# Seven inner products for P4 of the last output block in a pooling mixer

## The chip, the cores and the metric

The kernel runs on one core of a Trainium2 chip, as one launch. The metric is the device time of one execution in microseconds.

## The reference

The model is one layer of a streaming encoder trunk for x of 4096 rows and 1024 columns, float32. With one layer only the pooling mixer is used, not the gated attention:

```python
normed = rms_norm(x, norm_w)
u, gate = split(normed @ in_w, 2)                 # in_w 1024 x 2048
pooled = trailing means of u (windows 2, 4, 8, 16 for the four column groups) - u
mixed = einsum('bsgc,gcd->bsgd', pooled, group_w) + group_b
y = mixed * scale * silu(gate)
h = x + y @ out_w                                 # out_w 1024 x 1024
out = rms_norm(h, final_norm_w)
```

The change touches only `y @ out_w` for the last 512 rows.

## The kernel before

**Arithmetic.** All large matrix products are done with numbers split in two parts (a high part rounded to the matmul's input type, and the rest), as three matmuls: high by high, high by low, low by high. `split` (L232) makes the two parts with an ACT copy and a DVE subtraction; `copy` (L227) and `on_vector` (L213) are the helpers whose lines L229 and L215 stand in the profile for all such work.

**Stages.** A first stage folds weights together. Then come the phases "a" and "b" (the input projection in two column halves, four blocks of 1024 rows), with pooling beside them, and then the output phase "o", eight blocks (0 to 7) of 512 rows. Every block of every phase is a product of 2 x 2 blocks in Strassen's way with seven products P1 to P7 in place of eight. In the output phase their order is P1, P7, P6, P2, P5, P4, P3 (`ORDER_OUT`, L39), and each product multiplies 256 rows of some sum of quarters of y by a 512 x 512 sum of quarters of `out_w`, kept split in `w[i]`.

**A plain product.** `product_out` (L864) does two row halves of 128 rows (j = 0, 1). Each has four blocks of the contracted dimension and three matmuls for each, with 512 columns moving: 24 matmuls, all through `mm3` (L783).

**An inner product.** For the products named in `INNER` (L32), from one block to another, the same product is once more cut in 2 x 2 and done as seven inner products: A11 B11, A12 B21, S4 B22, A22 T4, S1 T1, S2 T2, S3 T3. The left sums S1 to S4 are made in phase "b" and kept in DRAM (`inner_sums`, `sumd`); the right sums T1 to T4 are made once (`inner_rights`, `split_inner`). T1 to T3 lie in buffers of their own. T4 is written over the quarter B12 (A22 B22's partner that the seven products don't need) of `w[i][0]`. Each inner product is six matmuls with 256 columns moving (`mm_inner`, L967, matmul on L972). The first, A11 B11, is issued by `inner_first` (L985) between the row halves of the product ahead, and ACT copies its result to a second bank. `inner_rest` (L992) issues the other six, and then adds the shared parts to the output rows with six `add_quarter` (L978, DVE on L980, 128 x 256 each), ahead of the ordinary eviction. For the shared parts P4 uses the two PSUM banks in which P1 and P2 were summed, once P2 is evicted; P2 uses the two spare banks.

Before the change `INNER` says that P2 is done so in blocks 1 to 7 and P4 in blocks 2 to 6. In block 7 P4 is a plain product and needs its quarter B12 back in place of T4. So behind P1 of block 7 `load_b12` (L912) loads it from DRAM, and behind P6 `split_b12` (L917) splits it into its place:

```python
def split_b12(i):
    src, t = raw_quarter(i, 0, 1), b12_place(i)
    for k in range(2):
        copy(t[:, 0, k], src[k])
        sub(t[:, 1, k], src[k], t[:, 0, k].bitcast(F32))
    give(inner_w[i].pop(("raw", 0)))
```

**What runs ahead.** `steps` lists all products. At step n the loads for up to step n + 4 are issued (`load_reach`, `load_o` L1182), and the left operands are formed and split for up to step n + 2 (`split_reach` L1698, `split_o` L1205). An inner P4 is an exception: its left side is split only one step ahead, and with it the sums S1 to S4, which `load_o` has loaded when it came to P3's step. A plain left side takes one of four `ops` buffers in turn, an inner one two of them. The order of instructions on each engine comes from a scheduler, which may put later work of the program ahead of work that isn't ready; the code above only sets priorities and dependencies.

**Buffers.** Rows and sums lie in two pools of equal tiles (`st`, `vt`), and `take` hands out the one given back longest ago; a new load waits until the old content has been read.

**The end.** `evict_o` (L1355) adds a product from PSUM to the rows x (L1373, DVE, one for each row half). In blocks 0 to 6 the row norm is computed behind P4 and P3 by `square_rows`. In block 7 it is done in parts to shorten the end: behind P2 and P5 `early_half` squares half rows on ACT (L1303) and multiplies them by the final weight on DVE, and behind P4 and P3 `square_part`, `late_factor` (root on ACT, L1321; small DVE operations, L1296 and L1324 to L1326), `late_scalar` (ACT, L1335) and `late_vector` (DVE, L1345) finish the rows and send them. P4 completes one 256-row half of the block (two groups of 128 rows), and P3 the other. P3's second row half is done in two column halves, the last one in a spare bank.

Of the kernel before, what the change touches and what calls it, by code (L numbers as in the profile page):

```python
# [28 lines left out]
NV = 8  # L29
EPS = 1e-6  # L30
FIRST_INNER = 1
INNER = {2: (1, 7), 4: (2, 6)}  # L32
INNER_IN = (0,)
STORED = {3: (0, 1, 2, 3)}

P1, P2, P3, P4, P5, P6, P7 = range(1, 8)
# [56 lines left out]
def kernel(  # L93
# [138 lines left out]
    def split(dst, src):  # L232
# [15 lines left out]
    wid = {  # L248
        i: [dram.tile([P, 2, H], F32, name=f"wid{i}_{n}") for n in range(2)] for i in INNER
    }  # L250
# [88 lines left out]
    def store_weights(dst, h, b11, b21, b12, b22):  # L339
        nc.sync.dma_start(out=dst[P1][h], in_=b11)  # L340
        nc.sync.dma_start(out=dst[P2][h], in_=b21)
        if h and P2 in INNER and dst is wod:
            inner_rights(P2, b21)
        for i, u in combine(b11, b21, b12, b22).items():
            nc.sync.dma_start(out=dst[i][h], in_=u)
            if h and i in INNER and dst is wod:
                inner_rights(i, u)
# [77 lines left out]
    def inner_rights(i, low):  # L425

        high, more = take(), take()
        nc.sync.dma_start(out=high, in_=wod[i][0])
        b11, b12, b21, b22, t4, t2 = (
            u.rearrange("p k (s a) -> p k s a", s=2)[:, :, :, c * QW : (c + 1) * QW] for u in (high, low, more) for c in range(2)  # L430
        )
        sub(b11, b12, b11)
        sub(b12, b22, b12)
        sub(t2, b22, b11)
        sub(t4, b21, t2)
        for n, u in enumerate((high, more)):
            nc.sync.dma_start(out=wid[i][n], in_=u)
            give(u)
# [454 lines left out]
    def is_inner(b, i):  # L893
        return i in INNER and INNER[i][0] <= b <= INNER[i][1]

    inner_w = {i: {} for i in INNER}

# [807 lines left out]
    def row_plan(b):  # L1705
# [19 lines left out]
        (2, P7): [(split_inner, P4, "T3")],  # L1725
        (2, P6): [(split_inner, P4, "T2")],
        (2, P2): [(split_inner, P4, "T4"), (end_inner, P4)],
        (7, P1): [(load_b12, P4)],
        (7, P6): [(split_b12, P4)],
    }  # L1730

    for n in range(2, len(steps)):
# [163 lines left out]
```

## Time and profile before

| | us |
|---|---|
| median of three runs | 906.63 |
| lowest and highest run | 905.44, 909.16 |
| the profiled execution's own time | 905.18 |
| its span, from the first to the last instruction | 903.4 |

PE is TensorE's matmuls, PEld its weight loads, DVE VectorE, ACT ScalarE, POOL GpSimd, and SP the engine that issues most transfers. A row of a timeline gives the start and the duration in microseconds, the engine, the line, the operation with what it writes and reads, how many of them, and in brackets how long the engine had been idle before it and what ended that. A row of the chain of waits gives start, duration and what the chain ran through. A row of a table by windows gives, for each stretch, its length, the busy time of PE, PEld, DVE, ACT and POOL with their numbers of instructions, the granted TensorE clock as a share of full speed, the busy share of the DMA engines and GB/s. A row of the list of transfers gives what is written from what, the queue, how many, the size of each, and the median time from issue to landing.

Matmuls are pipelined, so the durations of single ones overlap; what a group of them costs is read from where the next group starts.

### The profile page before, as it was taken

What the parts mean: (1) busy time and instruction counts of PE and PEld (TensorE: products, weight loads), DVE (VectorE), ACT (ScalarE), POOL (GpSimd) and SP (SyncE); (2) the same over time, 40 slices, a digit from 0 to 9 for tenths busy, and PEclk for the clock granted to TensorE, in tenths of its full rate; (3) what the DMA queues carried; (4) which work ended last, traced back from release to release, by engine and by line L of the source; (5) the groups of instructions that cost most, each with busy time, mean ns of one, the idle gap of its engine ahead of it and who ended that gap; (6) DMA issues with size and microseconds to landing.
All of it is one profiled execution on the core that took longest, in us unless ns stands there. A gap on an engine that the chain in (4) does not pass through costs nothing.

```text
span 903.4 us, 12068 instructions
## 1 busy us (share of the span) xinstructions
PE 895.7 (99%) x4482; PEld 790.3 (87%) x4482; DVE 776.2 (86%) x973; ACT 487.6 (54%) x807; POOL 42.0 (5%) x75
## 2 busy tenths in 40 slices
PE   9999999999999999999999999999999999999997
PEld 7888888888888888898888888888898998999996
DVE  5999994894998998699589589799999989889897
ACT  6979547447346556355445545654446435355354
POOL 0023101101100000000000000000100000000000
PEclk9999999999999999999999999999999999999999
DMA  9986966956856844056826866855875584584652
GB/s 349 408 320 198 347 221 193 316 187 230 335 207 228 280 146 140 24 154 225 326 89 224 331 236 215 291 194 190 278 254 203 188 308 147 180 279 158 216 187 94
DMA packets 75148, 205.40 MB, mean 227 GB/s; under 512 B 6928, under 2 KB 29840, under 8 KB 75088
## 3 DMA queue, kind: packets, MB, share of 16 engines
q1 hardware_dynamic: 67440, 179.17, 56.3%
q10 hardware_dynamic: 5040, 16.79, 5.0%
q0 software_dynamic: 2608, 8.66, 2.7%
q8 instruction: 35, 0.57, 0.3%
q14 instruction: 25, 0.20, 0.1%
HBM read 130.13 MB, written 74.46 MB: 226 GB/s over the span
## 4 chain that ended last, share of the span: by engine, by line
PE 98%; DVE 1%; ACT 0%; issue 0%; DVEq 0%; ACTq 0%
PE bank L783 87%; PE bank L972 6%; PE bank L497 3%; PE bank L816 1%; PE bank L1485 0%; DVE op L215 0%; DVE w L215 0%; DVE st L215 0%; PE bank L563 0%; ACT vt L1303 0%; DVE st L1373 0%; DVE st L1345 0%; ACT vt L1335 0%; ACT vt L229 0%; DVEq L1892 0%
## 5 line engine op out<-in xcount | busy, mean ns | idle before, releaser
L783 PE MATMUL bank<-op,w 128*128 128x512 f32 x2640 | 571.4, 379 | 0.2
L783 PEld LDWEIGHTS bank<-op,w 128*128 128x128 f32 x2640 | 498.4, 189 | 72.3 <-DVE op L215 1.0
L783 PE MATMUL bank<-w,op 128*128 128x512 f32 (+1 forms) x1068 | 232.2, 377 | 0.0
L783 PEld LDWEIGHTS bank<-w,op 128*128 128x128 f32 x1068 | 198.3, 189 | 26.9 <-issue 0.2
L215 DVE TENSOR_TENSOR op<-st,op 128x1024 fp32r<-128x1024 f32 x79 | 95.2, 1209 | 28.5 <-ACT op L229 28.3
L229 ACT ACTIVATE op<-st 128x1024 fp32r<-128x1024 f32 x79 | 82.4, 1048 | 57.5 <-PE bank L783 45.0
L229 ACT ACTIVATE op<-vt 128x1024 fp32r<-128x1024 f32 x69 | 71.8, 1052 | 58.4 <-PE bank L783 32.4
L215 DVE TENSOR_TENSOR op<-vt,op 128x1024 fp32r<-128x1024 f32 x69 | 83.6, 1215 | 10.4 <-ACT op L229 10.3
L229 ACT ACTIVATE vt<-bank 128x512 f32<-128x512 f32 x94 | 53.2, 590 | 44.3 <-PE bank L783 32.5
L229 ACT ACTIVATE bank<-bank 128x512 f32<-128x512 f32 (+1 forms) x76 | 38.0, 502 | 63.4 <-PE bank L783 32.1
L215 DVE TENSOR_TENSOR op<-s_st,op 128x1024 fp32r<-128x1024 f32 x31 | 37.6, 1217 | 12.0 <-ACT op L229 12.0
L229 ACT ACTIVATE op<-s_st 128x1024 fp32r<-128x1024 f32 x31 | 32.4, 1049 | 21.9 <-PE bank L783 11.8
L1373 DVE TENSOR_TENSOR vt<-bank,vt 128x512 f32<-128x512 f32 x56 | 37.9, 680 | 3.3 <-PE bank L783 3.3
L972 PE MATMUL bank<-w,op 128*128 128x256 f32 x288 | 40.0, 275 | 0.0
L972 PEld LDWEIGHTS bank<-w,op 128*128 128x128 f32 x288 | 37.8, 192 | 1.3
L215 DVE TENSOR_TENSOR vt<-bank,vt 128x512 f32<-128x512 f32 x50 | 32.7, 683 | 6.9 <-PE bank L783 6.8
L1237 POOL TENSOR_SCALAR oms<-oss 128x2 f32<-128x2 f32 x14 | 9.8, 696 | 615.4 <-ACT st L1264 443.2
L1070 DVE TENSOR_TENSOR_SCAN vt<-vt,bf 128x512 f32<-128x512 f32 x28 | 34.4, 1267 | 1.3 <-ACT vt L229 1.3
L215 DVE TENSOR_TENSOR w<-st,w 128x1024 fp32r<-128x1024 f32 (+2 forms) x25 | 28.1, 1132 | 8.5 <-ACT w L229 8.5
L229 ACT ACTIVATE w<-st 128x1024 fp32r<-128x1024 f32 (+2 forms) x25 | 24.2, 984 | 18.8 <-DMA st<-wod 9.0
L215 DVE TENSOR_TENSOR vt<-vt,vt 128x1024 f32<-128x1024 f32 (+1 forms) x29 | 33.0, 1140 | 0.1
L229 ACT ACTIVATE st<-bank 128x512 f32<-128x512 f32 x34 | 20.0, 594 | 24.0 <-PE bank L783 16.2
(171 smaller groups left out, 817.9 us busy)
## 6 DMA issues: line engine op xcount, KB each, us to landing
st<-in_x SPq DMA_DIRECT2D x27, 512.0 KB, 5.8
st<-in_xt SPq DMA_DIRECT2D x27, 512.0 KB, 8.9
vt<-in_x SPq DMA_DIRECT2D x27, 512.0 KB, 5.0
sd<-st ACTq DMA_DIRECT2D x27, 512.0 KB, 5.6
vt<-yd SPq DMA_DIRECT2D x18, 512.0 KB, 5.6
st<-sd SPq DMA_DIRECT2D x17, 512.0 KB, 5.4
out<-vt SPq DMA_DIRECT2D x17, 512.0 KB, 3.5
yd<-st SPq DMA_DIRECT2D x16, 512.0 KB, 2.9
```

Of the source, the lines that this page charges most:

```text
L215: made.append(nc.vector.tensor_tensor(out=dst, in0=a, in1=b, op=op))
L229: made.append(nc.scalar.activation(dst, src, func, **how))
L497: latest[0] = nc.tensor.matmul(ps2[kk][:, j * 256 : (j + 1) * 256], a[:, kk, 2 * j + t, :], maps if len(pairs) == 1 else woven(maps), star ...
L783: latest[0] = nc.tensor.matmul(ps, a, b, start=start and n == 0, stop=stop and n == 2, skip_group_check=True).ins
L816: latest[0] = nc.tensor.matmul(quarter_bank(banks_[c], n), a[:, x_, k, c * P : (c + 1) * P], right[:, y_, k], start=start and k + m == 0, ...
L972: latest[0] = nc.tensor.matmul(dst, a[k][x_], b[k][y_], start=start and k + n == 0, stop=k == 1 and n == 2, skip_group_check=True,).ins
L1070: nc.vector.tensor_tensor_scan(s[:, j, at:end], v[:, j, at:end], v[:, j, at - win : end - win], sums_of[j] if sums_of else 0.0, ALU.add, A ...
L1237: nc.gpsimd.tensor_scalar(out=ms, in0=ss, scalar1=-0.5 / D, scalar2=-0.5 * EPS, op0=ALU.mult, op1=ALU.add)
L1373: partial["added"] = nc.vector.tensor_tensor(out=dst, in0=src, in1=dst, op=ALU.add).ins
```

## The change

P4 of block 7 is done as seven inner products too, like P4 of blocks 2 to 6, and the load and the split of its quarter B12 are left out, since nothing reads that quarter any more.

```diff
-INNER = {2: (1, 7), 4: (2, 6)}
+INNER = {2: (1, 7), 4: (2, 7)}
...
         (2, P2): [(split_inner, P4, "T4"), (end_inner, P4)],
-        (7, P1): [(load_b12, P4)],
-        (7, P6): [(split_b12, P4)],
     }
```

By `is_inner(7, P4)`, which is now true, four more things follow in block 7: `load_o` loads S1 to S4 for P4, `split_o` splits them into a second `ops` buffer, `split_reach` lets P4's left side be split one step ahead in place of two, and P5's `product_out` issues `inner_first` between its row halves. The rest, from `evict_o` on, is the same code. Blocks 0 to 6 are the same.

## The prediction

> **What bounds the kernel now.** I read the page first, for the share of each engine, then the chain of waits for the stretch that the change touches, and then the timeline of VectorE (DVE) and ScalarE (ACT) in that stretch.
>
> ```profile
> span 903.4 us, 12068 instructions
> ...
> PE 895.7 (99%) x4482; PEld 790.3 (87%) x4482; DVE 776.2 (86%) x973; ACT 487.6 (54%) x807; POOL 42.0 (5%) x75
> ```
>
> TensorE (PE) is busy for 99% of the span, so a matmul taken out is worth its full time as long as nothing new makes PE wait, and as long as what follows the last matmul doesn't grow. The span is 903.4 us in an execution whose own time is 905.18 us; the median of the three runs is 906.63 us, 1.45 us above that execution. I make the sum as a difference and put it on the median.
>
> The end of the chain of waits shows both parts of the last output block, the matmuls and what comes after them.
>
> ```profile
> 873.75 0.67 PE bank L972 x6
> 874.42 2.59 PE bank L783 x12
> 877.01 4.02 PE bank L972 x36
> 881.03 12.97 PE bank L783 x60
> 893.99 0.02 issue
> 894.02 0.70 DVE st L1373
> ...
> 894.74 0.73 ACT vt L1303 x2
> ...
> 898.80 0.35 DVE s_st L1345
> ```
>
> Columns are start, duration, engine and line. L972 is the inner form (six matmuls 256 wide for each inner product), L783 the plain one (512 wide). The 60 plain matmuls from 881.03 are P5 (24), P4 (24) and the first row half of P3 (12). There the chain leaves PE: from 893.99 to the last DVE operation at 898.80 the kernel waits for evictions, squares and scales, not for matmuls, though the second row half of P3 still runs. So this block has two limits: PE up to the middle of P3, and DVE with ACT after it. The change is good for the first and must be weighed in the second.
>
> **The matmuls.** Twelve plain matmuls take 2.59 us (874.42), so P4 now costs 2 x 2.59 = 5.18 us. As inner products it costs 0.67 us (the first product, put between the row halves of P5) and 4.02 us (the other six), 4.69 us by the rows at 873.75 and 877.01. Saved: 5.18 - 4.69 = **0.49 us**. With these prices the new PE clock reads: P5's first row half ends at 881.03 + 2.59 = 883.62, the first inner product at 884.29, P5 at 886.88, P4 at 890.90 and P3's first row half at 893.49 instead of 893.99.
>
> A 256-wide matmul costs slightly more than half of a 512-wide one here (4.02/36 = 112 ns against 2.59/12 = 216 ns), and that it pays at all hangs on this. The Trainium skill, TensorE: Matmul & The Clock Gate, section Back-to-back issue gap, speaks against it: it says that in a stream of weight loads and matmuls the spacing is about 81 ns at 128 columns and 131 ns at 512. Interpolated, that gives an estimate of 98 ns at 256, so 42 x 98 against 24 x 131 ns, 0.97 us lost in place of 0.49 us gained, and a sum 1.46 us higher than mine. The rows above have both widths in the same stream and contradict it, so I give it no weight.
>
> **What is left out.** The load of the weight quarter (one transfer of 512 KB on SP's queue) and its split, two ACT copies and two DVE subtractions.
>
> ```profile
> 871.04 0.72 ACT L229 ACTIVATE w<-vt 128x256 fp32r<-128x256 f32 x2 [4.41 <-DMA vt<-wod]
> 871.55 1.53 SPq L1278 DMA_DIRECT2D out<-vt  x2
> ```
>
> The copies take 0.72 us on an ACT that had been idle for 4.41 us waiting for that very transfer, and the chain holds nothing but PE there, so leaving all of it out gains nothing that ends last. I take zero; if DVE were behind, the two subtractions would be worth as much as two of the 128x256 adds below, under 0.9 us.
>
> **What is added before P4: the sums S1 to S4.** One load of 512 KB, one ACT copy and one DVE subtraction of 128x1024. The load is issued at the P6 step, four steps ahead. By the order in which buffers are given back it gets the buffer of one of block 6's output rows, which are sent at 871.55 (second row above); it cannot start before that transfer has read it. The page and the list of transfers give the medians of such a store and of such a load:
>
> ```profile
> out<-vt SPq DMA_DIRECT2D x17, 512.0 KB, 3.5
> ...
> vt<-sumd SPq DMA_DIRECT2D x9, 512.0 KB, 4.4
> ```
>
> So it can start at about 871.6 + 3.5 = 875.1 and land at 875.1 + 4.4 = 879.5. Behind it on SP's queue are only the final stores, so nobody else waits. The split of A11 to A22 also moves, from two steps ahead to one. The ACT rows of blocks 6 and 7 show what that does:
>
> ```profile
> 841.55 1.07 ACT L229 ACTIVATE op<-vt 128x1024 fp32r<-128x1024 f32 x1 [2.01 <-PE bank L783]
> ...
> 845.00 1.06 ACT L229 ACTIVATE op<-vt 128x1024 fp32r<-128x1024 f32 x1 [1.53 <-PE bank L972]
> ```
>
> ```profile
> 876.83 1.06 ACT L229 ACTIVATE op<-vt 128x1024 fp32r<-128x1024 f32 x1 [1.72 <-PE bank L783]
> ...
> 880.33 1.06 ACT L229 ACTIVATE op<-vt 128x1024 fp32r<-128x1024 f32 x1 [1.58 <-PE bank L972]
> 883.18 0.63 ACT L1303 ACTIVATE vt<-st 128x512 f32<-128x512 f32 x1 [1.79 <-DVE st L1373]
> ...
> 885.29 0.63 ACT L1303 ACTIVATE vt<-s_st 128x512 f32<-128x512 f32 x1 [1.39 <-issue]
> ...
> 890.08 0.63 ACT L1303 ACTIVATE vt<-vt 128x512 f32<-128x512 f32 x1 [1.54 <-DVE vt L1373]
> ...
> 892.21 0.64 ACT L1303 ACTIVATE vt<-vt 128x512 f32<-128x512 f32 x1 [1.08 <-DVE vt L1373]
> ...
> 894.74 0.64 ACT L1303 ACTIVATE vt<-st 128x512 f32<-128x512 f32 x1 [0.86 <-DVE st L1373]
> ...
> 895.50 0.30 ACT L1321 ACTIVATE columns<-columns 128x1 f32<-128x1 f32 x1
> 895.70 0.71 ACT L1335 ACTIVATE vt<-vt,columns 128x512 f32<-128x512 f32 x1
> 896.31 0.40 ACT L1303 ACTIVATE vt<-s_st 128x256 f32<-128x256 f32 x1
> ...
> 896.83 0.72 ACT L1335 ACTIVATE st<-st,columns 128x512 f32<-128x512 f32 x1
> 897.48 0.42 ACT L1303 ACTIVATE vt<-s_st 128x256 f32<-128x256 f32 x1
> ```
>
> Block 6 has the late split (P4 is inner there), block 7 the early one, and yet the copy of P4's left side stands 35.28 us apart, as the blocks do: at 841.55 and 876.83, each released by the end of P6. The scheduler has put it ahead of P2 although the code has it behind. So I expect it at 876.8 again. The copy of the sums takes the place at 880.33 (block 6: 845.00), and P3's copy follows. The sums are first read at 886.88 + 0.67 = 887.55; copied by 881.4 and subtracted on DVE behind P2's first eviction (block 7's own subtraction below ends at 884.6), they have 2.9 us to spare. PE should not stall: cost zero before P4 ends, and past 2.9 us of lateness what is above it.
>
> **What is added behind P4: six quarter adds.** Here DVE's rows in block 7, with P2 as the pattern of an inner product that is not followed by another block's work:
>
> ```profile
> 879.72 0.42 DVE L980 TENSOR_TENSOR st<-bank,st 128x256 f32<-128x256 f32 x1 [0.57 <-PE bank L972]
> 881.13 0.42 DVE L980 TENSOR_TENSOR st<-bank,st 128x256 f32<-128x256 f32 x1 [0.98 <-PE bank L972]
> ...
> 882.47 0.68 DVE L1373 TENSOR_TENSOR st<-bank,st 128x512 f32<-128x512 f32 x1
> 883.07 0.41 DVE L980 TENSOR_TENSOR s_st<-bank,s_st 128x256 f32<-128x256 f32 x1
> 883.40 1.21 DVE L215 TENSOR_TENSOR op<-vt,op 128x1024 fp32r<-128x1024 f32 x1
> 884.53 0.68 DVE L1373 TENSOR_TENSOR s_st<-bank,s_st 128x512 f32<-128x512 f32 x1
> ...
> 888.71 0.68 DVE L215 TENSOR_TENSOR vt<-vt,s_st 128x512 f32<-128x512 f32 x1
> ...
> 889.31 0.68 DVE L1373 TENSOR_TENSOR vt<-bank,vt 128x512 f32<-128x512 f32 x1
> ...
> 891.50 0.68 DVE L1373 TENSOR_TENSOR vt<-bank,vt 128x512 f32<-128x512 f32 x1
> 892.10 0.74 DVE L1345 SCALAR_TENSOR_TENSOR vt<-vt,columns,s_st 128x512 f32<-128x512 f32 x1
> ...
> 894.02 0.69 DVE L1373 TENSOR_TENSOR st<-bank,st 128x512 f32<-128x512 f32 x1 [0.30 <-PE bank L783]
> ```
>
> The first add goes before the last product, the second only 0.10 us after the product ends (881.03). Four adds take 881.13 to 882.47, 1.34 us; an eviction takes 0.60 us to the next start, the last add 0.33 us, a 128x1024 subtraction 1.13 us. In P4 that means: adds from 891.00, first eviction at 892.34 (now 889.31), last add at 892.94, second eviction at 893.27 to 893.87 (now 891.50). So **P4's two rows come out of PSUM 3.03 and 1.77 us later than now, in spite of a PE that is 0.49 us ahead.** The extra subtraction of the sums shifts DVE's work on P2 and P5 by 1.13 us, and now that work runs from 881.13 up to 889.31 with no idle time on any row, so it would run to 890.44; with the one add that may go early, 890.8. That still ends before 891.00.
>
> What is late next is ACT. Start-to-start prices from its rows: a 512-wide square with its read-out 0.76 us (894.74 to 895.50), a root 0.20, a scale 0.61 (895.70 to 896.31) or 0.65 (896.83 to 897.48), a 256-wide square 0.52. P4's squares begin at 892.34 + 0.71 = 893.05, 2.97 us after 890.08. From there ACT has, back to back, square, root, square, root and scale of P4 (0.76 + 0.20 + 0.76 + 0.20 + 0.61 = 2.53), P3's first square and root (0.96), P4's second scale (0.61), a 256-wide square (0.52) and P3's first scale (0.65): 893.05 + 5.27 = 898.32 for the last square, which now starts at 897.48. **Later by 0.84 us.** DVE in the same stretch has P4's first scaling (0.74 us, now at 892.10) behind 893.87; if it gets ahead of P3's evictions, its time comes on top, 0.84 + 0.74 = 1.6. So between +0.8 and +1.6; I take +0.9, near ACT's end, since the scheduler has so far put evictions first (894.02, ahead of P4's second scaling). The 0.49 us of PE is already inside these numbers, since every start was worked out from the new PE clock. The bounds: -0.49 us if the scheduler sorts the tail so well that it keeps its length, and +2.7 us if nothing of the added DVE work is absorbed (1.13 + 1.34 + 2 x 0.33 = 3.1 less 0.49).
>
> Sum: 906.63 + 0.9 = **907.5 us** (for a profiled execution like the one shown, 905.18 + 0.9 = 906.1). That is 0.1%, and about 0.5%, 4.5 us, is what a measurement of this kernel can tell from no change.
>
> **The rivals.** *The tail keeps its length*: squares and scales of P4 and P3 are interleaved so that P3's eviction, due 0.50 us earlier, isn't delayed; then all of the 0.49 us arrives, 906.1 us. For it speaks that DVE and ACT have idle time after 889 (ACT waits 1.54, 1.08 and 0.86 us in the rows above); against it, that all of that idle time lies before P4's rows would now be ready. *The late split really is late*: if in block 7 the scheduler leaves P4's left side where the code has it, behind P2's two squares, its copy starts at 885.29 + 0.76 = 886.05 and is there at 887.1, its low half 1.2 us later, while PE wants both from 883.62. PE then stands for 3.5 to 4.7 us, and with the tail the sum is 911.0 to 912.2 us, slower than before. It decides from the moment at which that copy ends after 883.62. Against it stands the row at 841.55; for it, that block 6 has no squares behind P2. Here is what the clock does when PE has little to do:
>
> ```profile
> 894.00:903.40 9.40, 2.66 (x24) 2.46 (x23) 5.04 (x16) 4.21 (x11) 0.00 (x0) 0.81 0.57 212
> ```
>
> After the last matmuls the granted clock falls to a mean of 0.81. The Trainium skill (same page, HAM oscillation) says that a gap of over about 3.4 us makes the next work start at half rate; by that the stall would cost an estimated 1.7 us more. No stall of that length lies between matmuls here. *DVE runs over*: the +2.7 us bound, 909.3 us, if the adds wait in DVE's queue ahead of P5's evictions. *No effect* is not possible: the six matmuls are gone or the output is another.
>
> **How the numbers follow.** Forecast, the tail a little longer than the gain: 0.62. Tail keeps its length: 0.24. DVE runs over: 0.08. Late split: 0.06. The first three lie within 0.5% of 906.63, so within 0.5% has 0.92 after a little scatter, slower 0.06; faster by 4.5 us has no mechanism, PE can give only a tenth of it, and I leave 0.02 for scatter. Range: the lower end is the lowest run less the full gain, 905.44 - 0.49, about 905.0; the upper is 909.3 with some of the scatter of the runs shown, 910.0. Late split lies outside.
>
> **What would show it.** Right: PE without a wait through P5 and P4, 42 matmuls of L972 more and 24 of L783 less; P4's first eviction at about 892.3 and its first square at about 893.05; ACT without gaps from there; the last square near 898.3. Wrong: the copy of P4's left side after 883.6 or a wait of PE, which is the late split; P3's first eviction at 893.5 with the last square before 897.5, which is the tail that keeps its length.

## The result and the profile after

| | before | after |
|---|---|---|
| median of 22 runs, us | 905.50 | 907.49 |
| lowest and highest run, us | 904.60, 909.32 | 906.34, 912.10 |
| profiled execution, us | 905.18 | 910.08 |
| its span, us | 903.4 | 908.3 |

The ratio is 1.0022, with a 95% interval from 1.0014 to 1.0031: about 2 us slower, clear of the noise, but less than the 0.5% that the prediction took as the least that tells from no change. The forecast was 907.5 with a range of 905.0 to 910.0.

The page of after first, then its waits of PE:

```profile
span 908.3 us, 12112 instructions
...
PE 895.7 (99%) x4500; PEld 790.6 (87%) x4500; DVE 778.5 (86%) x978; ACT 487.9 (54%) x808; POOL 42.4 (5%) x75
```

```profile
PE bank L783 <- DVE op L215: 1.3, 1, 1.3
PE bank L783 <- ACT bank L229: 1.2, 1, 1.2
```

The chains of waits of after and of before place those waits; both pieces begin at the same matmul of phase "b":

```profile
573.88 90.73 PE bank L783 x419
```

```profile
570.85 90.72 PE bank L783 x419
```

There are 18 more matmuls (42 more on L972, 24 fewer on L783). The span is 4.9 us longer, but not all of that belongs to the change: 3.03 us of it had gone by 574 us. Most of that is the two waits above, both in phase "b", whose code is the same in both kernels: 1.3 us up to 573.88 for a left side, and 1.2 us up to 555.25 for a copy into a PSUM bank. The trace of before has neither, and a second profile of after has only the one for the left side. In the experiments below that one takes anything from nothing (e5 and e6, which have the change) to 2.7 us (e3), and 1.1 us in e4, which doesn't have the change; so nothing ties it to the change. Therefore stretches are compared here from one event in block 7: the start of P5's first matmul in the chain, 881.03 us before and 884.05 us after. What lies ahead of it is 3.02 us longer in this one execution; subtract 3.02 to put a time of after on the clock that the prediction used.

The chain of waits of after, its end:

```profile
884.05 2.59 PE bank L783 x12
886.65 0.67 PE bank L972 x6
887.31 2.59 PE bank L783 x12
889.91 4.02 PE bank L972 x36
893.92 2.61 PE bank L783 x12
896.53 0.02 issue
896.55 0.69 DVE st L1373
...
897.44 0.60 DVE vt L1373
898.04 0.02 issue
898.06 0.73 ACT vt L1303 x2
...
903.70 0.35 DVE s_st L1345
```

PE runs from P5 into P3 without a wait. P3's first row half ends at 896.53, which is 893.51 on the old clock where before had 893.99: PE's half microsecond did arrive. Behind it the last DVE scaling starts at 903.70, 19.65 us after P5's first matmul; before, 898.80 - 881.03 = 17.77. Call this stretch the **tail**. It grew by **1.88 us**, and the medians differ by 1.99 (by the interval, 1.3 to 2.8), so the tail accounts for the loss as far as the times can tell.

The timeline of DVE shows where in the tail:

```profile
892.98 0.42 DVE L980 TENSOR_TENSOR vt<-bank,vt 128x256 f32<-128x256 f32 x1
...
893.37 0.68 DVE L215 TENSOR_TENSOR vt<-vt,s_st 128x512 f32<-128x512 f32 x1
893.97 1.41 DVE L980 TENSOR_TENSOR vt<-bank,vt 128x256 f32<-128x256 f32 x4
895.30 0.68 DVE L1373 TENSOR_TENSOR vt<-bank,vt 128x512 f32<-128x512 f32 x1
895.90 0.41 DVE L980 TENSOR_TENSOR vt<-bank,vt 128x256 f32<-128x256 f32 x1
896.55 0.69 DVE L1373 TENSOR_TENSOR st<-bank,st 128x512 f32<-128x512 f32 x1 [0.24 <-PE bank L783]
...
897.35 0.67 DVE L1373 TENSOR_TENSOR vt<-bank,vt 128x512 f32<-128x512 f32 x1
```

and the timeline of ACT what hangs on it:

```profile
896.07 0.63 ACT L1303 ACTIVATE vt<-vt 128x512 f32<-128x512 f32 x1 [3.04 <-DVE vt L1373]
...
898.06 0.63 ACT L1303 ACTIVATE vt<-vt 128x512 f32<-128x512 f32 x1 [0.94 <-DVE vt L1373]
...
899.63 0.61 ACT L1303 ACTIVATE vt<-st 128x512 f32<-128x512 f32 x1
...
902.39 0.40 ACT L1303 ACTIVATE vt<-s_st 128x256 f32<-128x256 f32 x1
```

The row at 896.55 writes `st`: it is the eviction of P3's first rows. It stands **ahead** of P4's second eviction (897.35, `vt`). DVE first idles 0.24 us for PE, then evicts P3, and only then P4's second rows, which could have come out directly behind the add of 895.90. ACT keeps the other order: P4's second square (898.06), then P3's (899.63). So P3's early eviction lies ready and unused, and ACT idles 0.94 us in front of the square it wants.

### The profile page after: what moved, and what is told of

Same layout as the page of the kernel before. It is cut to its first block, busy times and chain, and to the rows that moved or that the text cites. A ratio compares the mean times of both kernels' runs of the same rounds, so it can differ in the third digit from the quotient of the medians.

```text
span 908.3 us, 12112 instructions
## 1 busy us (share of the span) xinstructions
PE 895.7 (99%) x4500; PEld 790.6 (87%) x4500; DVE 778.5 (86%) x978; ACT 487.9 (54%) x808; POOL 42.4 (5%) x75
## 4 chain that ended last, share of the span: by engine, by line
PE 95%; DVE 3%; issue 1%; ACT 1%; DVEq 0%; ACTq 0%
PE bank L783 83%; PE bank L972 7%; PE bank L497 3%; PE bank L816 1%; DVE op L215 1%; DVE w L215 1%; DVE st L215 1%; DVE vt L1070 1%; PE bank L1485 0%; DVE vt L1092 0%; DVE vt L215 0%; ACT vt L1303 0%; PE bank L563 0%; ACT vt L1335 0%; DVE s_st L215 0%
## 5 line engine op out<-in xcount | busy, mean ns | idle before, releaser
L783 PE MATMUL bank<-op,w 128*128 128x512 f32 x2640 | 571.6, 379 | 2.7 <-DVE op L215 1.3
L783 PEld LDWEIGHTS bank<-op,w 128*128 128x128 f32 x2640 | 498.3, 189 | 75.2 <-DVE op L215 2.2
L783 PE MATMUL bank<-w,op 128*128 128x512 f32 (+1 forms) x1044 | 227.3, 377 | 0.0
L783 PEld LDWEIGHTS bank<-w,op 128*128 128x128 f32 x1044 | 193.6, 189 | 26.1 <-issue 0.2
L215 DVE TENSOR_TENSOR op<-st,op 128x1024 fp32r<-128x1024 f32 x79 | 95.3, 1210 | 28.9 <-ACT op L229 28.7
L215 DVE TENSOR_TENSOR op<-vt,op 128x1024 fp32r<-128x1024 f32 x70 | 84.9, 1217 | 10.4 <-ACT op L229 10.3
L215 DVE TENSOR_TENSOR op<-s_st,op 128x1024 fp32r<-128x1024 f32 x31 | 37.7, 1218 | 13.2 <-ACT op L229 13.2
L972 PE MATMUL bank<-w,op 128*128 128x256 f32 x312 | 43.3, 275 | 0.0
L972 PEld LDWEIGHTS bank<-w,op 128*128 128x128 f32 x312 | 41.0, 192 | 1.4
L215 DVE TENSOR_TENSOR vt<-bank,vt 128x512 f32<-128x512 f32 x50 | 32.8, 684 | 6.9 <-PE bank L783 6.8
L215 DVE TENSOR_TENSOR w<-st,w 128x1024 fp32r<-128x1024 f32 (+2 forms) x25 | 28.1, 1132 | 8.5 <-ACT w L229 8.5
L215 DVE TENSOR_TENSOR vt<-vt,vt 128x1024 f32<-128x1024 f32 (+1 forms) x29 | 33.0, 1141 | 0.0
L215 DVE TENSOR_TENSOR st<-st,vt 128x1024 f32<-128x1024 f32 (+1 forms) x28 | 32.6, 1198 | 0.4 <-DMA vt<-rd 0.4
```

The source lines that it names most:

```text
L215: made.append(nc.vector.tensor_tensor(out=dst, in0=a, in1=b, op=op))
L783: latest[0] = nc.tensor.matmul(ps, a, b, start=start and n == 0, stop=stop and n == 2, skip_group_check=True).ins
L972: latest[0] = nc.tensor.matmul(dst, a[k][x_], b[k][y_], start=start and k + n == 0, stop=k == 1 and n == 2, skip_group_check=True,).ins
```

## The experiments

All were run in five rounds beside the kernel before. The next table has, for each, the times from the profile, counted from P5's first matmul (in microseconds; the start of an operation each): the group in which the four middle quarter adds lie, P4's two evictions, P3's first eviction, and the last scaling, which is the tail.

| kernel | adds | P4 first | P4 second | P3 first | tail | median (before beside it) | ratio, 95% |
|---|---|---|---|---|---|---|---|
| before | - | 8.28 | 10.47 | 12.99 | 17.77 | 905.50 | 1 |
| after | 9.92 | 11.25 | 13.30 | 12.50 | 19.65 | 907.49 (905.50) | 1.0022, 1.0014 to 1.0031 |
| e1_order | 9.92 | 11.25 | 12.29 | 13.19 | 18.80 | 906.62 (905.98) | 1.0005, 0.9990 to 1.0020 |
| e2_shared_first | 9.51 | 11.39 | 12.52 | 13.34 | 19.02 | 906.88 (905.98) | 1.0012, 1.0000 to 1.0024 |
| e3_no_adds | - | 8.92 | 10.18 | 12.72 | 17.50 | 906.16 (905.98) | 1.0002, 0.9987 to 1.0017 |
| e4_no_b12 | - | 8.28 | 10.47 | 12.99 | 18.03 | 906.73 (905.98) | 1.0008, 0.9996 to 1.0020 |
| e5_pool_order | 9.98 | 11.31 | 12.36 | 13.25 | 18.91 | 907.00 (906.44) | 1.0005, 0.9992 to 1.0018 |
| e6_pool_shared | 8.58 | 9.92 | 11.03 | 13.20 | 18.00 | 906.58 (906.44) | 1.0004, 0.9989 to 1.0019 |
| e8_before_pool | - | 7.81 | 10.40 | 12.99 | 17.78 | 906.37 (906.44) | 1.0003, 0.9987 to 1.0018 |
| e9_late_scaling | 8.58 | 9.91 | 11.03 | 12.51 | 17.90 | 906.05 (905.92) | 0.9997, 0.9982 to 1.0012 |
| after_again | 9.92 | 11.25 | 13.30 | 12.50 | 19.65 | 907.76 (905.92) | 1.0030, 1.0016 to 1.0043 |

After and its repeat agree in the tail to 0.01 us; the other kernels have one profile each, so their tails are taken as equally steady, which is not shown. The intervals of the times are 1.5 to 2.8 us wide. Verdicts below therefore rest on the tail; every change of the tail lies within the interval of the times, but after's alone is clear of no change in them.

**e1_order: P3's eviction behind P4's second.**

```diff
-                partial["added"] = nc.vector.tensor_tensor(
-                    out=dst, in0=src, in1=dst, op=ALU.add
-                ).ins
+                first_p3 = final and i == P3 and j == 0
+                with tc.issue_after(partial["added"]) if first_p3 else nullcontext():
+                    partial["added"] = nc.vector.tensor_tensor(
+                        out=dst, in0=src, in1=dst, op=ALU.add
+                    ).ins
```

> The changed kernel, with one constraint more: P3's first eviction (DVE, block 7) is issued behind P4's second one. Measure: the tail, from the end of P2's inner products on PE to the start of the last DVE scaling; 17.77 us before (881.03 to 898.80), 19.65 us in the changed kernel (884.05 to 903.70). Theory A (order): the changed kernel's DVE takes P3's first eviction ahead of P4's second one, so that ACT's second square of P4 starts 1.03 us later than its data allowed; with the order mended the tail is 18.6 us and the time some 1.0 us below the changed kernel's, 0.9 us over before's. Rival B (amount): DVE is simply behind by the work added, the order only shifts it around, and the tail stays at 19.4 to 19.8 us.

DVE's timeline, P5's first matmul being at 881.19:

```profile
892.44 0.68 DVE L1375 TENSOR_TENSOR vt<-bank,vt 128x512 f32<-128x512 f32 x1
893.04 0.41 DVE L980 TENSOR_TENSOR vt<-bank,vt 128x256 f32<-128x256 f32 x1
893.48 0.69 DVE L1375 TENSOR_TENSOR vt<-bank,vt 128x512 f32<-128x512 f32 x1
...
894.38 0.67 DVE L1375 TENSOR_TENSOR st<-bank,st 128x512 f32<-128x512 f32 x1
```

P4's second eviction comes 12.29 us after P5's start instead of 13.30, P3's 0.69 later than in after, and the tail is 0.85 us shorter: 18.80. So 0.85 of the 1.88 us were the order of two evictions. A tail of 18.6 was expected for that, and 19.4 to 19.8 if the amount of work alone counted. What is left, 1.03 us over before, is close to the +0.9 that the prediction had for evictions in the right order.

**e3_no_adds: after without P4's six adds in block 7.** Everything else of the change stays.

```diff
         mm_inner(i, t, "S3", "T3", z[1][1], False)
+        if b == NBO - 1 and i == P4:
+            return
         add_quarter(us, 0, 0, z[0][0])
```

> The changed kernel without the six quarter adds behind block 7's P4, so that the shared parts are missing from those rows of the output; inner products, sums, their split and everything else stay. If the adds are what makes the tail longer: tail 17.77 less the 0.49 us of PE, 17.2 to 17.4 us, and a time 0.4 to 0.6 us below before's. Rival C (the split of the sums, 1.13 us of DVE ahead of P4, or the later split of P4's left side is what costs): the tail stays over 18.3 us.

```profile
894.16 0.68 DVE L1375 TENSOR_TENSOR vt<-bank,vt 128x512 f32<-128x512 f32 x1
...
895.42 0.69 DVE L1375 TENSOR_TENSOR vt<-bank,vt 128x512 f32<-128x512 f32 x1
...
896.71 0.75 DVE L1347 SCALAR_TENSOR_TENSOR vt<-vt,columns,s_st 128x512 f32<-128x512 f32 x1
...
897.96 0.68 DVE L1375 TENSOR_TENSOR st<-bank,st 128x512 f32<-128x512 f32 x1
```

The tail is 17.50 us, 0.27 shorter than before and just above the 17.2 to 17.4 expected; the time (906.16 against 905.98) can't tell. The adds, with the order they bring, thus cost 19.65 - 17.50 = 2.15 us, and without them the change gives 0.27 of PE's 0.49. The rest stays on DVE: P3's first eviction (897.96) stands behind P4's scaling and small operations, 12.72 us after P5's start, where the same eviction in after waits for PE alone and has 12.50. From that eviction to the last scaling it takes 4.78 us, in before too (898.80 - 894.02).

**e2_shared_first: the products that are shared go first in P4,** S2T2, S1T1, A12B21, S3T3, then the six adds, then S4B22 and A22T4.

```diff
         in_turn[0] = None
+        if b == NBO - 1 and i == P4:
+            mm_inner(i, t, "S2", "T2", z[1][0], False)
+            copy(z[1][1], z[1][0])
+            mm_inner(i, t, "S1", "T1", z[0][1], True)
+            mm_inner(i, t, "A12", "B21", to[0][0], False)
+            mm_inner(i, t, "S3", "T3", z[1][1], False)
...
+            mm_inner(i, t, "S4", "B22", to[0][1], False)
+            mm_inner(i, t, "A22", "T4", to[1][0], False)
+            return
```

> The changed kernel, with block 7's P4 inner products in another order: S2 T2, S1 T1, A12 B21, S3 T3 first, then S4 B22 and A22 T4, and the six quarter adds written ahead of these two. The shared parts are complete 1.34 us earlier on PE. Theory A with late products (the four adds waited for S3 T3): P4's evictions come up to 1.3 us earlier and the tail is 17.5 to 18.2 us. Rival B (DVE is busy with older work until the adds anyway, up to 9.92 us after P2's end, where S3 T3 ended 9.86 us after it): the adds start no earlier than in the changed kernel, and only what the order gives can be had, 18.5 to 18.7 us. If nothing changes at all, 19.6 us, the order is not the cause either.

It was meant to let the adds start while PE still works on P4, and it hardly did. DVE had other work up to then:

```profile
890.55 0.68 DVE L215 TENSOR_TENSOR vt<-vt,s_st 128x512 f32<-128x512 f32 x1
891.15 1.74 DVE L980 TENSOR_TENSOR vt<-bank,vt 128x256 f32<-128x256 f32 x5
893.03 0.69 DVE L1388 TENSOR_TENSOR vt<-bank,vt 128x512 f32<-128x512 f32 x1
```

The adds start directly behind the last multiplication of `early_half` (L215), almost 1 us after S3T3 ended on PE (8.53 us after P5's start, by PE's rows), and the first eviction is no earlier than in after. The tail, 19.02, is in none of the expected ranges. It is shorter than after's by something not intended: with this order of the program the scheduler left P3's eviction behind P4's second. That the last shared product alone holds the adds up is refuted.

**e5_pool_order: e1, and the four multiplications of `early_half` on GpSimd.** It takes the other suspected holder, DVE's backlog, away and leaves the products as they are.

```diff
-        mul(u, u, fw[0][:, n])
+        nc.gpsimd.tensor_tensor(out=u, in0=u, in1=fw[0][:, n], op=ALU.mult)
```

> e1_order, with the four multiplications by the final weight behind P2 and P5 of block 7 (128x512 each, 0.60 us of DVE to the next start) given to POOL, so that DVE has 2.4 us less ahead of P4's adds. Tail as before (P2's end to the start of the last scaling): e1_order had 18.80 us. Theory E (two limits meet: DVE's older work ended 9.92 us after P2's end, the last shared product S3 T3 9.86 us after it): freeing DVE alone gains nothing, since four of the six adds still wait for S3 T3; tail 18.6 to 18.9 us. Rival B (DVE's amount of work alone is the limit): the adds start up to 2.4 us earlier and the tail is 17.3 to 17.8 us.

```profile
885.34 1.64 DVE L215 TENSOR_TENSOR op<-vt,op 128x1024 fp32r<-128x1024 f32 x1
...
889.75 0.42 DVE L980 TENSOR_TENSOR vt<-bank,vt 128x256 f32<-128x256 f32 x1 [0.35 <-PE bank L972]
891.16 1.42 DVE L980 TENSOR_TENSOR vt<-bank,vt 128x256 f32<-128x256 f32 x4 [0.99 <-PE bank L972]
```

Now DVE idles 0.99 us for PE in front of the four adds, and they start 9.98 us after P5's first matmul, no earlier than in after. So after meets **two limits at the same moment**: PE ends P4's last product, S3T3, 9.87 us after P5's start (893.92 in the chain of after), and DVE comes free at 9.92. Taking either away alone (e2, e5) shows the other. The tail is 18.91, at the upper end of the 18.6 to 18.9 expected, and no shorter than e1's.

**e6_pool_shared: both at once** (e2 with the multiplications on GpSimd), **and e8_before_pool, its control** (before with them there).

> e2_shared_first, with the four multiplications on POOL as well: both limits are lifted. Theory E: the six adds are done by the time the last product ends (9.86 us after P2's end), P4's evictions start about 9.7 and 10.3 us after P2's end against 11.25 and 13.3 in the changed kernel, ACT has its squares ahead of P3's first eviction again, and only the 0.49 us of PE is left: tail 17.2 to 17.5 us, time 0.3 to 0.6 us below before's and 2 us below the changed kernel's. Rival B: as in the run with POOL and the other order, no better than that one. Rival F (ACT's extra work, or POOL's slow multiplications, limits anyway): over 18 us.

> The kernel before with the four multiplications on POOL, a control for the other two: DVE had idle time ahead of P4's and P3's evictions there, so nothing should change, tail 17.6 to 17.9 us and time within 0.3 us. If POOL helps here too, by more than 0.4 us, the gain of the two runs beside it is not the inner products' own.

DVE's timeline of e6, P5 starting at 881.54:

```profile
890.12 1.42 DVE L980 TENSOR_TENSOR vt<-bank,vt 128x256 f32<-128x256 f32 x4 [0.20 <-PE bank L972]
...
893.87 0.75 DVE L1360 SCALAR_TENSOR_TENSOR vt<-vt,columns,s_st 128x512 f32<-128x512 f32 x1
...
894.74 0.67 DVE L1388 TENSOR_TENSOR st<-bank,st 128x512 f32<-128x512 f32 x1
```

The adds start 1.34 us earlier and the tail falls to 18.00. That is 1.65 below after, and 0.80 below e1, which has the evictions in the right order as e6 has. The control didn't move (17.78), so that gain is not GpSimd's by itself. But 17.2 to 17.5 was expected. P3's first eviction waits behind P4's scaling of 893.87, so that PE's half microsecond is lost once more.

**e9_late_scaling: e6 with that scaling put off behind P3's eviction.**

```diff
-                        late_vector(half, 0, n, factors[0])
+                        partial["first"] = (half, 0, n, factors[0])
                         partial["waiting"] = (half, 1, n, factors.pop())
                     else:
+                        late_vector(*partial.pop("first"))
```

> e6_pool_shared, with DVE's scaling of P4's first rows (0.75 us) written behind P3's first eviction in place of ahead of it. In e6_pool_shared that eviction stood at 13.36 us after P2's end (P5's first matmul), though its matmuls were done at about 12.66, because the scaling stood ahead of it; ACT's square behind it waited 0.47 us. Theory A (order on DVE in the last microseconds): the eviction moves to 12.7 us, the square by 0.4 to 0.5 us, and the tail from 17.99 to 17.4-17.6 us, below the 17.77 us of before; time 0.2 to 0.4 us below before's, too little for the times to show. Rival F (ACT, whose copies and squares are the same, limits): the tail stays at 17.9 to 18.1 us.

```profile
894.16 0.69 DVE L1388 TENSOR_TENSOR st<-bank,st 128x512 f32<-128x512 f32 x1 [0.21 <-PE bank L783]
...
899.55 0.88 DVE L1360 SCALAR_TENSOR_TENSOR s_st<-s_st,columns,s_st 128x128 f32<-128x128 f32 x2
```

```profile
896.31 0.72 ACT L1350 ACTIVATE vt<-vt,columns 128x512 f32<-128x512 f32 x1 [0.23 <-DVE columns L1341]
...
897.62 0.72 ACT L1350 ACTIVATE st<-st,columns 128x512 f32<-128x512 f32 x1 [0.19 <-DVE columns L1341]
```

The eviction now waits for PE alone and stands 12.51 us after P5's start, 0.48 earlier than in before. Even so, the tail is 17.90, a miss against the 17.4 to 17.6 expected. From that eviction to the last scaling it takes 5.39 us in place of 4.78, and 0.42 of these 0.61 us are two waits of ACT for the small operations that make the factors (second fence). That these are late because the scaling that was put off now stands between them is read from DVE's order and was not tested. This is the best version with all inner products and adds in P4; its time is within 0.03% of before (0.9997, 0.9982 to 1.0012). No version was measurably faster than before.

**e4_no_b12: before without the load and split of the quarter.** P4 of block 7 stays plain and multiplies T4 in its place.

```diff
-        (7, P1): [(load_b12, P4)],
-        (7, P6): [(split_b12, P4)],
```

> The kernel before, with only the load and the split of the weight quarter left out, so that P4 of block 7 multiplies T4 in place of B12. My account puts this at zero: tail 17.7 to 17.85 us, time within 0.3 us of before's. Rival D (the freed transfer and copies help or the changed buffers hurt): the tail moves by more than 0.2 us or the time by more than 0.5 us.

The evictions stand where they stood in before, to 0.01 us, but the tail is 0.26 us longer, where 0 was expected. ACT's timeline has the spot:

```profile
898.31 0.72 ACT L1335 ACTIVATE st<-st,columns 128x512 f32<-128x512 f32 x1 [0.32 <-DVE columns L1296]
```

In before this scale (896.83) had no wait. The operations of the tail have the same order in both programs on DVE and ACT. The program hands out one buffer less, so the squares should write to another one, but the trace doesn't name buffers. Why the scale waits for one more small DVE operation is open. In after the same scale starts at 901.77, directly behind ACT's operation before it, so nothing shows that this loss is a part of the 1.88 us.

**after_again** repeats after unchanged, beside e9.

> The changed kernel once more, beside e9_late_scaling on the same chip. Its tail was 19.65 us in one execution, 1.88 us over before's; all theories expect 19.5 to 19.8 us again, if the order on the engines and not an accident of that execution makes it, and a time 1.3 to 2.5 us above before's.

Every entry of its row agrees with that of after, and its ratio (1.0030) lies in the interval of the first.

## Why the prediction was right or wrong

**The number was right partly by chance.** The sum was made on 906.63 us, the median of three runs of before; over 22 runs that is 905.50. The base was 1.1 us too high and the difference 1.1 us too small (+0.9 forecast, +1.99 measured), and the two cancel. The sign and the place of the loss, a tail that grows by more than PE gains, were as forecast; its size was not.

Point by point, times of after on the old clock:

- **PE's 0.49 us: right.** P5's first half, the first product and the six others took 2.59, 0.67 and 4.02 us, the prices it used. The Trainium skill's spacing (TensorE: Matmul & The Clock Gate, Back-to-back issue gap), by which the inner form would lose, is not what these 42 added matmuls show, at 112 ns each.
- **No wait of PE, A11 split early: right.** The split's copy started at 876.84 (forecast 876.8) and the sums' copy at 880.34 (880.33). The rival *late split* is out.
- **P4's first eviction and square: right.** 892.28 and 893.05, against 892.34 and 893.05. DVE was free of its backlog at 890.95 (forecast 890.8), 0.05 us after S3T3 ended. So the rival *DVE runs over* is out as well, with less than 0.1 us to spare: the four adds had been forecast for 891.00.
- **P4's second eviction: wrong, and this is the step that failed.** Forecast 893.27, measured 894.33. The prediction said that "the scheduler has so far put evictions first", and took the lower end of its 0.8 to 1.6 us for that reason. It asked whether a *scaling* would get ahead of an *eviction*, and not which of two evictions would be first. The second square came at 895.04 instead of 894.01 (893.05 + 0.76 + 0.20), and the last square at 899.37 instead of 898.32: about the same 1.05 us, handed on. "ACT without gaps from there" failed with it (0.94 us idle). The bound of 1.6 was exceeded too, by 0.3 us. e1 puts the step right and gives 0.85 us of it back.
- **The remaining +0.9: about right.** With the order mended, e1 has +1.03. The price of the adds held too: the four took 1.33 us (893.97 to 895.30), against 1.34.
- **The quarter's load and split at zero: off by the little that can be seen alone.** Leaving them out of before cost 0.26 us in the tail (e4), by a wait whose cause is open; the prediction had bounded it as a gain only.
- **The rival *tail keeps its length*: not in after,** though nearly in e9 (+0.13). It took a new order of products, DVE's multiplications elsewhere and one scaling put off.
- **Two readings beside the sum.** The clock of 0.81 was called that after the last matmuls, but its row starts at 894.00, while PE still works: from 894.00 to 896.70 the granted clock is 1.00, and from there to the end it is 0.74 in the mean. And "the six matmuls are gone", said of *no effect*, isn't so: 24 plain matmuls give way to 42 inner ones. Neither enters the forecast.

## What to carry to other kernels

At the end of a kernel, cost a change by the moment at which each result leaves PSUM and by what the engines behind it still have to do in order, not by the matmuls saved: here 0.49 us of PE bought 2.15 us of adds and waits. Write out the static order of each engine there, for two results that come nearly together, and see whether the next engine wants them in the same order; evicting first the one that the consumer wanted second cost 0.85 us here. And when two limits end at the same moment, an experiment that removes one of them can look like a refutation of it (e2 and e5 here): remove both before you drop either.

## What the runs showed of the hardware

DVE and GpSimd slow each other. GpSimd's multiplications of 128x512 in e5, which read two operands:

```profile
884.14 1.77 POOL L1312 TENSOR_TENSOR st<-st,s_st 128x512 f32<-128x512 f32 x1 [19.21 <-ACT vt L1303]
886.25 1.88 POOL L1312 TENSOR_TENSOR s_st<-s_st,s_st 128x512 f32<-128x512 f32 x1 [0.34 <-ACT vt L1303]
888.53 2.52 POOL L1312 TENSOR_TENSOR vt<-vt,s_st 128x512 f32<-128x512 f32 x2 [0.41 <-ACT vt L1303]
```

Two in a row take 1.26 us each (888.53). The second (1.88) began while the DVE subtraction from 885.34 to 886.98 was running; in e8 no subtraction stood beside it:

```profile
884.08 1.77 POOL L1312 TENSOR_TENSOR st<-st,s_st 128x512 f32<-128x512 f32 x1 [19.22 <-ACT vt L1303]
886.19 1.29 POOL L1312 TENSOR_TENSOR s_st<-s_st,s_st 128x512 f32<-128x512 f32 x1 [0.34 <-ACT vt L1303]
```

That subtraction had itself begun while the first multiplication was running, and took 1.64 us in place of the 1.21 of such a one in before (883.40). The first multiplication took 1.77 us in both runs, so it isn't that subtraction which slows it. In both it began while an earlier subtraction was running, which kept its usual time; in e8:

```profile
883.49 1.22 DVE L215 TENSOR_TENSOR op<-vt,op 128x1024 fp32r<-128x1024 f32 x1
```

So in each of the three overlaps the operation that began later took longer. The first subtraction and the first multiplication lost nothing to what began behind them; for the second subtraction that can't be told. The first multiplication also followed 19 us without work on GpSimd, and no run tells whether that made it slow.

DVE does the same multiplication in 0.68 us. The Trainium skill, SBUF — State Buffer, section Who interferes with whom, says that a DVE instruction with two SBUF inputs contends with a GpSimd instruction that reads SBUF; the subtraction of 885.34 and the second multiplication agree with it, at a price of about 0.4 us for DVE and 0.6 for GpSimd.
